# A margin for overtaking products in the order emitter, state-space tables stored in eight parts, attention loads held back: a hybrid S5 and forgetting-attention layer on one core

## The chip, the core and the metric

The kernel runs on one core of one Trainium2 chip. The metric is the device time of one execution in microseconds (us); several executions of each kernel are timed and the median is given. Beside them one execution was recorded by the hardware profiler, and every duration below comes from that record.

## What is computed

One decoder layer over 2048 tokens of 1024 channels, in float32. A projection of the normalized, modulated input gives the inputs of two branches and their gates; the branches are merged, projected, and normalized once more:

```python
u = _layer_norm(h) * (1.0 + scale[:, None, :]) + shift[:, None, :]
proj = u @ w_in[l]
(x_ssm, z_ssm, q, k, v, f_logit, z_attn, g_ssm, g_attn) = jnp.split(proj, split_idx, axis=-1)
y_ssm = _s5_mixer(x_ssm, ...)                  # 32 groups of 16 channels, 64 complex states each
y_ssm = (y_ssm * jax.nn.silu(z_ssm)) @ w_proj_ssm[l]
log_f = jax.nn.log_sigmoid(f_logit + b_f[l]).transpose(0, 2, 1)
o = _forgetting_attention(to_heads(q), to_heads(k), to_heads(v), log_f)   # 8 heads of 64, causal
y_attn = (o * jax.nn.silu(z_attn)) @ w_proj_attn[l]
merged = jax.nn.sigmoid(g_ssm) * y_ssm + jax.nn.sigmoid(g_attn) * y_attn
sub = (merged @ w_out[l]) * gate[:, None, :]
h = _layer_norm(DEEPNORM_ALPHA * h + sub, ln_g[l], ln_b[l])
```

## The kernel before

Every large product is made of three products of float32r parts (high by high, high by low, low by high), each of 128 x 128 weights by up to 512 columns. The stages follow one another on TensorE (PE): the layer norm, the modulation and the first projection columns (phase 1a); the other projection columns (`projections`), beside which the state-space branch runs on the other engines; attention in 64 rounds (8 heads by 8 pairs of query blocks, `scores`, `exponentials`, `weights_times_v`, `normalize`), beside which the GLU and the state-space output product run as filler (`background`); then the merge, the output projection and the last layer norm.

No engine reorders its instructions, so the order in which the program emits them decides. It is chosen by a rough clock, class `Model`: it keeps a modelled time of each engine (`M.t`), of the DMA queue (`M.t["dma"]`, filled at 360 bytes per ns, line 133) and of each tile's last write and reads. Each stage is a Python generator, a stream, that yields the modelled time at which its next step could start. `Model.merge` (line 168) goes through the streams in order of rank and takes the first whose time is not past PE's modelled clock; where there is none it takes the earliest and moves PE's clock there. State space ranks first, then the exponentials, `weights_times_v`, `normalize`, `scores`, then the end stages, `background` and `output`, and `projections` last. The lowest ranks are thus what fills PE while the higher ones wait. `scores` also waits until `background` has had a share of its 64 jobs (`share`, with `AHEAD = 62.5`), and runs at most three rounds ahead of `weights_times_v`.

Three ways of emitting matter here. `Engine.when` gives the modelled time of a step's operands. `Engine.soon` yields that time and then emits. `Engine.later` puts an instruction on a held list, from which it is emitted once PE's modelled clock has reached the time of its operands, or earlier where something needs it; `sp.dma_start` without `later` is emitted at once, and the SyncE queue (SP) then stands until the transfer's semaphores are there, with all later transfers behind it.

The state-space tables of all 32 groups are built in one tile `pk` by `ssm_params`, stored to `pk_sc` by a single transfer (line 963) and read back a group at a time into `pkg` tiles by `stage_l` (line 988). `stage_a` makes from them `CA` (VectorE, DVE), `G` and the phase tables (GpSimd, POOL); the first product that needs these is in `stage_b`, into a `bg` bank. `projections` empties its four `pp` banks through two `st` tiles that ScalarE (ACT) writes, for the z columns VectorE too, and SP stores (`zs_sc<-st`).

Attention's operands come from `load_keys` (line 1202: `ks`, `fb` and `vs` of 512 keys, a ring of six) and `load_q` (line 1215: the queries of two rounds, a ring of two). `pools` (line 1236) loads two chunks of keys and the queries of rounds 0 and 1 early; the rest is asked for by `scores`.

Of the kernel before, what the change touches and what calls it, by code (L numbers as in the profile page):

```python
# [8 lines left out]
F32 = mybir.dt.float32  # L9
# [9 lines left out]
NW = 4          # token windows of 512  # L19
WT = 512  # L20
KD = D // 128
NG = 32         # state-space groups
GH = 16         # channels of a group
CL = 8          # tokens of a chunk
NCH = S // CL   # chunks
CW = WT // CL   # chunks of a window
# [10 lines left out]
PKN = 163       # of a group: Bbar 16 | swapped 16 | C 16 | swapped 16 | tables 64 | powers 19 | A^7..A^0 16  # L37
# [4 lines left out]
class Model:  # L42
    """A rough clock of the engines, by which the order of emission is chosen (it computes no data)."""

    # from the end of an instruction to the start, on another engine (or the same), of one that needs it
    LAT = dict(pe=dict(dve=230, act=270, pool=260, pe=0), dve=dict(pe=190, act=150, pool=130, dve=125),
               act=dict(pe=190, dve=198, pool=110, act=0), pool=dict(pe=190, dve=155, act=175, pool=100))

# [31 lines left out]
    def deps(self, e, kw):  # L80
        """When the operands are there for engine e (whose own accesses are in order)."""
        rd, wt = self.aps(kw)
        r = 0.0
        for n in rd:
            if n in self.wr:
                end, by = self.wr[n]
                r = max(r, end + self.lat(e, by))
            for h in self.held:
                if n in h[2]:           # (a transfer that is still to come)
                    r = max(r, max(h[0] + 1100, self.t["sp"] + 1100, self.t["dma"]) + 1700)  # L90
        for n in wt:
            for by, end in self.ac.get(n, {}).items():
                if by not in (e, "in") or (by == "in" and e != "sp"):
                    r = max(r, end + self.lat(e, by))
            if e == "sp":
                r = max(r, self.ac.get(n, {}).get("sp", 0.0) + self.lat(e, e))
        return r
# [36 lines left out]
    def run(self, e, op, kw):  # L134
# [11 lines left out]
        for n in wt:  # L146
            # parts of a tile that transfers fill do not wait for each other
# [3 lines left out]
    def settle(self, rd, wt, dma=False):  # L151
        """Emit what is held and has to come before a read of rd and a write of wt (transfers may fill parts of a
        tile in any order)."""
# [14 lines left out]
    def merge(self, streams):  # L168
        """Emit from the first stream whose next step would not wait; streams come in order of rank."""
# [8 lines left out]
        while live:  # L178
# [13 lines left out]
            self.t["pe"] = max(now, best[0])  # L192
# [4 lines left out]
class Engine:  # L197
    """An engine whose instructions the model sees."""
# [14 lines left out]
    def when(self, **kw):  # L213
        """When an instruction with these operands could start."""
        d = self.m.deps(self.name, kw)
        return d if self.name in ("pe", "sp") else max(d, self.m.t[self.name])

    def soon(self, op, /, **kw):
        """A stream's step: the instruction, emitted once it would not wait."""
# [3 lines left out]
    def later(self, op, /, **kw):  # L223
        """The instruction, emitted once its operands are there (the streams go on meanwhile)."""
# [6 lines left out]
def hybrid_layer(ctx: ExitStack, tc: tile.TileContext, x, c, w_ada, b_ada, w_in, b_f, lam_re, lam_im,  # L231
# [32 lines left out]
    def pround(o, i):  # L264
        """Pool's copy into float32r (its rounding)."""
# [19 lines left out]
    # maskb[q, k] = 0 where k <= q, NEG elsewhere  # L285
# [4 lines left out]
    # ------------------------------------------------------------------ phase 1: input projection  # L290
    esl = ExitStack()               # left: until the projection is done
# [11 lines left out]
    def ps_tile(n=[0]):  # L303
        """One of four banks, which attention later has for scores (three) and outputs."""
# [7 lines left out]
    def bg_tile(n=None):  # L312
        if n is not None and n % 4 > 1:         # (the banks of the transposes, once attention is done)
# [6 lines left out]
    def bank():  # L320
        """Whichever of the two banks of bg_tile is free."""
# [12 lines left out]
    def split_wide(raw, n):  # L334
        """A stream that splits a chunk of weights; the tiles are there at once."""
# [8 lines left out]
    def rstd_of(p, mv, n):  # L344
        """1 / sqrt(var + eps) of the variances mv[:, :, 1]."""
# [21 lines left out]
    def until(f):  # L367
        """A condition to wait on, whatever the time."""
        return lambda: 0.0 if f() else None

    def modulation():
        """shift | 1 + scale of silu(c) @ w_ada + b_ada, as columns, 128 channels at a time."""
# [3 lines left out]
        act.activation(out=one, in_=ident[:, 0:1], func=AF.Sqrt)    # (its table is there when the layer norm needs it)  # L376
# [43 lines left out]
    def early_keys():  # L420
        """Two column tiles of the keys' weights, with which the first window goes on while the next one comes."""
# [7 lines left out]
    def modulation_columns():  # L429
        """Sums over the partitions, as columns."""  # L430
# [17 lines left out]
    def column_sums(acc, n, c0):  # L448
        """mods[:, c0:] = sums of acc over its partitions, as columns, + b_ada."""
# [34 lines left out]
    def normalized():  # L484
        """Windows of tokens, less their mean and over their spread."""
# [21 lines left out]
    def modulated():  # L507
        """u = normalized * (1 + scale) + shift, channels on partitions."""
# [28 lines left out]
    def low_parts():  # L537
        """The two parts of u."""
# [23 lines left out]
    def products_of(ps, w, hi, lo, c0):  # L562
        """A tile of columns of the projection of a window."""
# [7 lines left out]
    def store_parts(kind, m, w, ps):  # L571
        """Queries (scaled) or keys, in two parts."""
# [92 lines left out]
    # the other columns, with the state-space branch alongside  # L665
# [55 lines left out]
    def forget_bias():  # L721
        """f_sc[h, t] = cumulative log_sigmoid(f + b_f)."""
        with ExitStack() as es:
# [10 lines left out]
            # log1p(e) = 2 artanh(s), s = e / (2 + e) <= 1/3  # L734
# [25 lines left out]
    def gate():  # L760
        """The gate part of the modulation, as a row (scaled by 1/16, which the merge leaves)."""
# [17 lines left out]
    def ssm_params():  # L779
        """Per group: input and output matrices, powers and phases, written to pk_sc."""  # L780
        with ExitStack() as es:
            p0 = pl(es, "spp", side="right")
            pk = p0.tile([128, NG, PKN], F32, name="pk")
            uv = p0.tile([128, 4, NG], F32, name="uv")    # phase of A^8 (cos, sin), zoh (re, im)
# [22 lines left out]
            # cosine and sine of arg = n pi/2 + r  # L807
# [21 lines left out]
            od, ev = t32(), t32()       # quadrant: odd * sign, even * sign  # L829
# [7 lines left out]
            def lin(o, p0_, q0, p1, q1, sub):  # L837
                """o = p0 q0 +- p1 q1"""
# [10 lines left out]
            # 0..8: real A^k, both halves; 9..17: imaginary A^k, [-; +]; 18: |A|^8; 19, 20: phase of A^8  # L849
# [4 lines left out]
            den, am, cr, ci = t32(), t32(), t32(), t32()      # zero-order hold  # L854
# [51 lines left out]
            # input matrix: Bbar = zoh * B, and with its halves swapped  # L906
            with ExitStack() as es2:
# [15 lines left out]
                # output matrix as [state, group, channel], and with its halves swapped  # L923
# [12 lines left out]
            # phase tables: cos, sin of phase * b and of phase * 16 a for a, b in 0..15  # L936
            ta_ = [p0.tile([128, NG, 8], F32, name=f"ta{i}") for i in range(2)]
            u_ = [p0.tile([128, NG], F32, name=f"u{i}") for i in range(2)]
            for cc, ss in ((64, 80), (96, 112)):
# [4 lines left out]
                while n < 16:  # L944
# [10 lines left out]
                    # double the phase  # L955
# [7 lines left out]
            sp.dma_start(out=pk_sc.rearrange("g p n -> p g n"), in_=pk)  # L963

    sq = dict(a=0, b=0, c=0, d=0, e=0, r=0, x=0, t=0, ready=False, st={})
    esss = ExitStack()

    def side():
        """What runs beside the projections, up to the state-space groups."""
# [18 lines left out]
    def stage_l():  # L988
        """Loads of each group."""
        yield until(lambda: sq["ready"])  # L990
        p = sq["p"]
        for g in range(NG):
# [3 lines left out]
            yield sp.when(out=pk, b=xr)  # L996
# [4 lines left out]
    def stage_a():  # L1001
        """Powered matrices and phase tables of each group."""
        yield until(lambda: sq["ready"])
        p, sign = sq["p"], sq["sign"]
        for g in range(NG):
# [21 lines left out]
            # C A^k: rows re = Cr Ar - Ci Ai, rows im = -(Ci Ar + Cr Ai)  # L1027
# [5 lines left out]
            # A^(7-j) Bbar  # L1033
# [19 lines left out]
    def stage_b():  # L1053
        """Stationary matrices and inputs of each group, split."""
# [44 lines left out]
    def stage_t():  # L1099
        """The matrix within a chunk, its columns put in the order of the output's rows."""  # L1100
# [20 lines left out]
    def stage_c():  # L1121
        """Chunk inputs, and the scan over chunks in a frame that turns with the phase."""
# [23 lines left out]
    def stage_r():  # L1146
        """The states before each chunk, turned back, split."""
# [20 lines left out]
    def stage_d():  # L1168
        """Outputs of each group: gelu, doubled."""
# [21 lines left out]
    # attention's inputs: chunks of 512 keys, loaded ahead  # L1191
# [4 lines left out]
    def ring(shape, dtype, tag, n, size, early, p0, p1):  # L1196
        """Tile n of a ring, whose first places are in a pool that is there earlier."""
# [4 lines left out]
    def load_keys():  # L1202
# [7 lines left out]
        sp.dma_start(out=f32(ks), in_=k_sc[h, :, :, tk].rearrange("a d t -> (a d) t"))  # L1210
        sp.dma_start(out=fb, in_=f_sc[h:h + 1, tk].to_broadcast([128, 512]))
        sp.dma_start(out=f32(vs), in_=v_sc[h, tk, :].rearrange("(n p) e -> p n e", p=128))
        at["k"][h, j], at["v"][h, j], at["f"][h, j] = ks, vs, fb

    def load_q():
        """The queries of two rounds, on both halves of the partitions."""
# [4 lines left out]
        for hf in range(2):  # L1221
            sp.dma_start(out=f32(qd[hf * 64:(hf + 1) * 64]),
# [3 lines left out]
    # ------------------------------------------------------------------ phase 2: attention beside the GLU and the  # L1226
    # projections; phase 3: merge, output projection, layer norm
    esat, esb = ExitStack(), ExitStack()

    def pools():  # L1230
        """The room of the input projection goes to attention, that of the state space to what runs beside it."""
# [16 lines left out]
        atp = pl(esat, "atp", side="right")  # L1248
        done["at"] = done["bg"] = True
# [3 lines left out]
    WR = 10         # places of the ring of weight chunks  # L1253
    WE = 2          # of these, in the earlier pool
    ZT = 3          # places of the ring of what products are combined with
    ck = dict(tiles={}, jobs=0)

    def weight_chunks():
        """The chunks of w_glu (gate and value in turn), w_proj_ssm and w_proj_attn, split."""
# [27 lines left out]
    def free_place(raws):  # L1287
        """Whether a load takes the place of the earlier pool."""
# [502 lines left out]
```

## Time and profile before

| | us |
|---|---|
| median of 3 runs | 1916.91 (1913.0 to 1919.92) |
| profiled execution, first to last instruction | 1913.3 |
| PE busy in it | 1833.8 |
| DVE, POOL, ACT busy | 1082.5, 923.6, 775.1 |

Matmuls are pipelined, so PE's busy time counts them at the rate at which they could follow each other. The difference between span and busy time is time in which PE stood. Beside it the record has the granted TensorE clock, which is 1.0 at 2.4 GHz and 0.5 at 1.2 GHz; a busy stretch at 0.5 does half the work.

### The profile page before, as it was taken

How to read it: one execution, taken by the hardware profiler on the slowest of the kernel's cores; microseconds unless marked ns; L12 is line 12 of the kernel's file. 1: busy time of each engine (PE TensorE's matmuls, PEld its weight loads, DVE VectorE, ACT ScalarE, POOL GpSimd, SP SyncE). 2: the span in 40 equal slices, each digit the busy share in tenths (PEclk: the TensorE clock that was granted, in tenths of full speed). 3: DMA queues.
4: the chain of work that ended last, by engine and by line, in shares of the span. 5: the costliest groups of instructions: out<-in, count | busy, mean ns of one | idle time of the engine just before them, and what ended most of it. 6: DMA issues, size and time to landing. Idle time of an engine off the chain costs nothing. (4 is left out here: it accounts for less than half of the span.)

```text
span 1913.3 us, 30538 instructions
## 1 busy us (share of the span) xinstructions
PE 1833.8 (96%) x10104; PEld 1565.5 (82%) x10104; DVE 1082.5 (57%) x2886; ACT 775.1 (41%) x1849; POOL 923.6 (48%) x1343
## 2 busy tenths in 40 slices
PE   4999999998999999999998999999999999899997
PEld 3789988886787888888887888988889888788886
DVE  8651114734555555552004777876777866567666
ACT  5441111121433444443114767876767866311110
POOL 5222111113889999995306566376543436533110
PEclk9899999998999999999998999999999999999999
DMA  9434346654333333335217365265364543744432
GB/s 302 138 86 119 94 110 183 149 133 121 101 94 105 100 105 97 105 101 138 91 50 189 98 169 140 77 183 152 113 201 131 151 137 127 260 146 136 131 123 89
DMA packets 276915, 252.37 MB, mean 132 GB/s; under 512 B 66396, under 2 KB 211828, under 8 KB 276756
## 3 DMA queue, kind: packets, MB, share of 16 engines
q1 hardware_dynamic: 276756, 250.41, 45.7%
q8 instruction: 80, 1.31, 0.3%
q14 instruction: 79, 0.65, 0.1%
HBM read 159.50 MB, written 86.63 MB: 129 GB/s over the span
## 5 line engine op out<-in xcount | busy, mean ns | idle before, releaser
L209 PE MATMUL pp<-uh,hi 128*128 128x512 f32 x1136 | 451.0, 397 | 0.0
L209 PE MATMUL pp<-uh,lo 128*128 128x512 f32 x1136 | 446.0, 393 | 0.0
L209 PE MATMUL pp<-ul,hi 128*128 128x512 f32 x1136 | 445.1, 392 | 0.0
L209 ACT ACTIVATE st<-pp 128x512 f32<-128x512 f32 (+2 forms) x168 | 93.9, 559 | 439.1 <-PE pp L209 383.4
L209 DVE TENSOR_TENSOR pl<-pt,ph 128x512 fp32r<-128x512 f32 (+1 forms) x288 | 183.3, 657 | 122.3 <-ACT ph L209 121.7
L209 PEld LDWEIGHTS pp<-uh,lo 128*128 128x128 f32 x1136 | 214.2, 189 | 46.3
L209 PEld LDWEIGHTS pp<-uh,hi 128*128 128x128 f32 x1136 | 216.4, 190 | 41.5
L209 PEld LDWEIGHTS pp<-ul,hi 128*128 128x128 f32 x1136 | 214.7, 189 | 41.9
L209 ACT ACTIVATE srow<-srow,nm 128x512 f32<-128x512 f32 (+2 forms) x320 | 207.6, 653 | 0.4 <-DVE nm L209 0.3
L209 ACT ACTIVATE ph<-pt 128x512 fp32r<-128x512 f32 (+1 forms) x288 | 159.8, 572 | 64.4 <-PE pt L209 51.6
L209 DVE CUSTOM_DVE_ANT_0 srow<-sc,fb 128x512 f32<-128x512 f32 (+3 forms) x288 | 163.0, 594 | 21.9 <-PE sc L209 21.9
L209 PE MATMUL sc<-ks,qd 128*128 128x512 f32 (+2 forms) x640 | 163.7, 381 | 7.1 <-DMA qd<-q_sc 7.1
L209 PE MATMUL pt<-ident,srow 128*128 128x128 f32 x1088 | 159.3, 275 | 8.7 <-DVE pl L209 4.7
L209 PE MATMUL acc<-ph,vs 128*128 128x256 f32 x576 | 163.0, 308 | 2.5 <-POOL ph L209 2.5
L209 POOL TENSOR_TENSOR oo<-oo 64x256 f32<-64x256 f32 x128 | 93.7, 732 | 143.0 <-ACT oo L209 140.0
L209 POOL TENSOR_SCALAR hi<-raw 128x512 fp32r<-128x512 f32 x60 | 39.9, 665 | 237.8 <-PE pp L209 191.7
L209 PEld LDWEIGHTS pt<-ident,srow 128*128 128x128 f32 x1088 | 128.4, 141 | 27.2 <-DVE pl L209 9.5
L209 PE MATMUL acc<-pl,vs 128*128 128x256 f32 x576 | 147.4, 282 | 0.5 <-DVE pl L209 0.5
L209 PE MATMUL bg<-bh,wh 128*128 128x512 f32 (+1 forms) x384 | 140.2, 365 | 5.1 <-DVE zt L209 5.1
L209 PE MATMUL bg<-bh,wl 128*128 128x512 f32 (+1 forms) x384 | 138.1, 360 | 0.0
L209 PE MATMUL bg<-bl,wh 128*128 128x512 f32 (+1 forms) x384 | 137.8, 359 | 0.0
L209 PEld LDWEIGHTS sc<-ks,qd 128*128 128x128 f32 x640 | 107.9, 193 | 24.4 <-issue 8.4
(240 smaller groups left out, 3811.3 us busy)
## 6 DMA issues: line engine op xcount, KB each, us to landing
xt<-in_x_dram SPq DMA_DIRECT2D x32, 512.0 KB, 3.7
qd<-q_sc SPq DMA_DIRECT2D x64, 256.0 KB, 5.4
raw<-in_w_in_dram SPq DMA_DIRECT2D x30, 512.0 KB, 4.5
wada<-in_w_ada_dram SPq DMA_DIRECT2D x16, 512.0 KB, 7.0
k_sc<-st SPq DMA_DIRECT2D x32, 256.0 KB, 3.3
v_sc<-st SPq DMA_DIRECT2D x32, 256.0 KB, 2.3
q_sc<-st SPq DMA_DIRECT2D x16, 512.0 KB, 3.3
gs_sc<-st SPq DMA_DIRECT2D x32, 256.0 KB, 2.3
```

The source lines that it names most:

```text
L209: return fn(kw["out"], 0.0) if op == "memset" else fn(**kw)
```

## The change

The diff also deletes comments and docstrings, which emits nothing. What is left has three parts.

```diff
+    MARGIN = 300.0
...
-            self.t["pe"] = max(now, best[0])
+            self.t["pe"] = max(now, best[0] - self.MARGIN)
...
     def when(self, **kw):
         d = self.m.deps(self.name, kw)
-        return d if self.name in ("pe", "sp") else max(d, self.m.t[self.name])
+        if self.name == "pe":
+            return d + self.m.MARGIN
+        return d if self.name == "sp" else max(d, self.m.t[self.name])
...
             yield sp.when(in_=pk)
-            sp.dma_start(out=pk_sc.rearrange("g p n -> p g n"), in_=pk)
+            for i in range(0, NG, PKG):
+                sp.dma_start(out=pk_sc[i:i + PKG].rearrange("g p n -> p g n"), in_=pk[:, i:i + PKG])
+                sq["stored"].append(M.t["dma"] + 2500)
...
+    PKG = 4
...
     def stage_l():
-            yield sp.when(out=pk, b=xr)
+            yield max(sp.when(out=pk, b=xr), sq["stored"][g // PKG])
+            M.t["sp"] = max(M.t["sp"], sq["stored"][g // PKG])
             sp.dma_start(out=pk, in_=pk_sc[g])
...
     def load_keys():
-        sp.dma_start(out=f32(ks), ...)
-        sp.dma_start(out=fb, ...)
-        sp.dma_start(out=f32(vs), ...)
+        sp.later("dma_start", out=f32(ks), ...)
+        sp.later("dma_start", out=fb, ...)
+        sp.later("dma_start", out=f32(vs), ...)
...
     def load_q():
-            sp.dma_start(out=f32(qd[hf * 64:(hf + 1) * 64]),
+            sp.later("dma_start", out=f32(qd[hf * 64:(hf + 1) * 64]),
...
     def pools():
         bgp = pl(esb, "bgp")
         atp = pl(esat, "atp", side="right")
+        load_q()
+        load_keys()
+        load_keys()
         done["at"] = done["bg"] = True
```

A step on PE is counted as ready 300 ns after its modelled operands; if no step of any stream is ready, the earliest is taken and PE's modelled clock moves to 300 ns before its yielded time, for a PE step to the operands' own time. The tables are stored by eight transfers of four groups, and a group's load is emitted only when the modelled clock says that its part has been stored for 2.5 us. The transfers of attention go on the held list, and `pools` asks for the queries of rounds 2 and 3 and for two more chunks of keys when the room for them opens.

## Rows read from the trace of the kernel before

**Rows 1.** Page, first part: busy time, share of the span, instructions.

```profile
PE 1833.8 (96%) x10104; PEld 1565.5 (82%) x10104; DVE 1082.5 (57%) x2886; ACT 775.1 (41%) x1849; POOL 923.6 (48%) x1343
```

**Rows 2.** Busy time by stretch; columns as its head says.

```profile
core 0: us, PE busy (x) PEld busy (x) DVE busy (x) ACT busy (x) POOL busy (x), PEclk, DMA share, GB/s
0.00:57.00 57.00, 29.00 (x127) 23.19 (x128) 49.10 (x88) 27.76 (x55) 29.82 (x39) 0.90 0.97 277
...
459.00:467.40 8.40, 0.91 (x5) 0.41 (x3) 2.63 (x4) 0.90 (x2) 5.74 (x10) 0.69 0.49 150
467.40:472.40 5.00, 4.92 (x13) 3.64 (x14) 1.51 (x5) 1.19 (x3) 2.88 (x6) 0.50 0.11 33
...
1033.60:1039.00 5.40, 5.33 (x16) 4.38 (x17) 2.92 (x12) 0.00 (x0) 3.51 (x5) 0.50 1.14 235
1039.00:1619.50 580.50, 563.04 (x3608) 496.55 (x3607) 432.69 (x1403) 414.12 (x1038) 315.07 (x483) 0.99 0.50 142
1619.50:1656.00 36.50, 27.55 (x182) 26.00 (x181) 19.61 (x31) 13.43 (x27) 27.22 (x27) 0.91 0.80 261
```

**Rows 3.** Timelines, 459 to 468 us: start, duration, instruction, idle time and releaser.

```profile
467.48 0.40 PE L209 MATMUL bg<-CA,pkg 128*16 128x128 f32 x1 [7.58 <-DVE CA L209]
...
464.73 0.69 DVE L209 SCALAR_TENSOR_TENSOR st<-st,pp 128x512 f32<-128x512 f32 x1 [12.99 <-ACT st L209]
...
461.29 0.41 POOL L209 TENSOR_TENSOR G<-pkg 128x128 f32<-128x128 f32 x1 [12.48 <-DMA pkg<-pk_sc]
```

**Rows 4.** Timeline of SP's queue, 444 to 466 us.

```profile
444.78 0.37 SPq L209 DMA_DIRECT2D pk_sc<-pk  x1
445.21 7.70 SPq L209 DMA_DIRECT2D dsk<-in_ssm_d_dram  x1
459.33 0.33 SPq L209 DMA_DIRECT2D pkg<-pk_sc  x1
...
461.19 4.58 SPq L209 DMA_DIRECT2D zs_sc<-st  x3
```

**Rows 5.** DMA issues, 440 to 470 us: count, size each, us to landing.

```profile
pk_sc<-pk SPq DMA_DIRECT2D x1, 2608.0 KB, 14.5
...
dsk<-in_ssm_d_dram SPq DMA_DIRECT2D x1, 2.0 KB, 14.3
```

**Rows 6.** From 1013 us: PE's waits to 1039, SP's timeline, DMA to 1035.

```profile
PE sc L209 <- DMA qd<-q_sc: 7.1, 2, 6.9
...
1026.69 1.26 SPq L209 DMA_DIRECT2D qd<-q_sc  x2
...
DMA packets 6289, 4.90 MB, mean 223 GB/s; under 512 B 2635, under 2 KB 4751, under 8 KB 6287
```

**Rows 7.** PE's waits, 1039 to 1619 us: total us, times, longest.

```profile
PE pt L209 <- DVE pl L209: 4.7, 6, 1.2
PE pt L209 <- ACT srow L209: 3.8, 2, 3.4
PE acc L209 <- DVE lb L209: 3.1, 4, 1.4
PE acc L209 <- POOL ph L209: 2.5, 1, 2.5
PE acc L209 <- ACT srow L209: 1.4, 1, 1.4
PE acc L209 <- DVE mx L209: 1.3, 1, 1.3
PE acc L209 <- DVE pl L209: 0.5, 1, 0.5
```

**Rows 8.** One of three stretches of attention at half clock; columns as in Rows 2.

```profile
1114.10:1117.50 3.40, 3.40 (x10) 2.74 (x9) 3.33 (x7) 2.05 (x5) 3.40 (x4) 0.50 0.73 163
```

**Rows 9.** SP's waits, 1039 to 1619 us: total us, times, longest.

```profile
SPq L209 <- PE sc L209: 10.8, 14, 4.8
```

**Rows 10.** Filler alone (tile bg), last eight rounds: PE, PEld, DVE, ACT busy, PEclk, DMA.

```profile
1546.40:1619.50 73.10, 25.15 (x91) 16.06 (x91) 5.42 (x8) 0.00 (x0) 0.98 0.48 145
```

## What the change will do to the time

> **What bounds the kernel now.** I read the page's first part first: PE is busy in 1833.8 of 1913.3 us [rows 1]. No other engine comes near, and the change takes no product away, so all it can win is the 79.5 us in which PE stands and the time it runs at half clock. The table by stretch then says where these are [rows 2]: 28.0 us before 57 us, 7.5 at 459 to 467, 6.9 at the start of attention [rows 6], 17.5 inside attention (580.50 less 563.04), 9.0 where the merge begins (36.50 less 27.55), and most of the rest behind the last product. From 57 to 459 us PE never stands, because a projection product with old operands is always at hand.
>
> Each long stand also has a stretch at half clock behind it. After the one at 459 us the clock is 0.50 until 472.4, so 5 us of busy PE do 2.5 us of work; after the one at the start of attention, 5.4 us do 2.7 [rows 2]. Inside attention there are three windows of 3.4 us at 0.50 [rows 8], up to 1.7 us lost in each, 5.1 together. The whole sum in reach of the three edits is then 7.6 + 2.5, 6.9 + 2.7, and 17.5 + 5.1, some 42 us or 2.2%. The waits of PE, in a third view, say who ends each, and that decides how much an edit reaches.
>
> **Part 1, the tables in parts.** PE stands 7.58 us for `CA` of the first group [rows 3]. SP tells why: the store is issued at 444.78 and lands 14.5 us later [rows 4, 5]; the first `pkg` load waits in SP until 459.33, and the stores of z columns stand behind it until 461.19 [rows 4]. So the `st` tiles are full, ACT and then DVE get to their `st` step late (464.73), and `CA` comes behind that on DVE although POOL has had `pkg` since 461.29 [rows 3]. The emitter charged the store 2608 KB at 360 bytes per ns, 7.4 us, half of what it took; that is how PE came to `CA` too early.
>
> The change adds seven DMA issues at 0.37 us each on SP [rows 4], 2.6 us, in front of the `dsk` load and the z stores; two `st` tiles and four banks cover that, and without the cover it would cost its 2.6 us. It does not bring the first tables by much. The 2 KB `dsk` load, issued behind the store and waiting for nothing of it, took 14.3 us [rows 5], so what is issued behind the parts arrives behind all eight, at about 459.5. What it does bring is that SP no longer stands: z stores issued before the load pass at once. Then `st` is free near 461 and `CA` need not wait for 464.73. Bounds of the gain in idle time: nearly nothing below (the load lands with two z stores of 256 KB ahead of it, about 1.4 us each at the store's 184 bytes per ns, so PE stops waiting at about 466: 1.5 us gained), and all 7.6 above. Between them, `pkg` near 461.5 to 462 and POOL's three and DVE's three steps of about 2 us put `CA` at 464. PE comes to it a little later than now, since the emitter adds 0.3 us and sees its load behind the z stores (0.7 us each by its own rate), at about 461. That leaves 3 us of standing: 4.6 gained. A stand of that size is followed by one window of 3.4 us at 0.50 in attention [rows 8], not by 5 us of it behind a longer idle stretch, so 0.8 more. Part 1: -5.4 us.
>
> The Trainium skill, page "DMA: Bandwidth & Descriptors", section "Queues, rings and completion order", says that each engine consumes the descriptors of a ring in order. By that the first part is stored early and its load is still served last, which speaks against most of what storing in parts could give. The `dsk` row is this trace's sign of it, 14.3 us for 2 KB. If instead the load could pass the other seven parts, the whole stand and its slow stretch would go, -10.1 in place of -5.4.
>
> **Part 2, attention loads.** Holding them back would help if SP stood for their room. In attention SP's waits that PE's score products end come to 10.8 us in all, 14 times [rows 9], and none of PE's waits there is ended by a DMA [rows 7]. So `later` itself is costed at nothing, bounds -1 and +1; its cover is the lead of the loads, three rounds, and without it a load costs the 6 to 7 us of the start. The new loads in `pools` are another thing. PE stands 6.9 us there for the queries of rounds 4 and 5, issued at 1026.69, and the DMA moved 4.90 MB in the 22 us around it at 223 GB/s [rows 6]: the queue is full. The queries of rounds 2 and 3 and the first of the two chunks come where they came before. The second chunk, 0.79 MB, moves ahead of the y loads, the weight chunks, the zs loads and those queries, on SP (some 1.4 us of issues) and in the DMA queue: 0.79 MB at 223 GB/s is 3.5 us later for all of them. The emitter knows it as 2.2 us and adds 0.3, so PE comes to round 4 about 2.5 us later: +1.0 us. Bounds: -7 if what fills those 2.5 us lets the rest arrive, +4.5 with no filler (the weights it needs are late as well) and a longer slow stretch.
>
> **Part 3, the margin.** Inside attention PE waits 16 times, 17.4 us in all, mostly for DVE or ACT steps that come 0.3 to 3.4 us after the emitter expects them [rows 7]. A step now goes ahead of lower ranks only 0.3 us later, and in between stand scores or filler. Taken at its own size the margin takes 0.3 us off each wait, nothing off those already shorter: about 5.1 us over the 16 (the small ones count 0.1 to 0.3). Of the three slow windows half should go with the shorter waits, 2.5. Part 3 in attention: -7.6 us. Bounds: all 22.6 above; below zero, +5, since a new order puts other steps together and its waits are drawn anew; nothing in the trace excludes that. I take the value near the margin's own size because a DVE wait of 0.78 us in the mean (4.7 over 6) is longer than what is added.
>
> Elsewhere the margin is costed at nothing. In the first 57 us nothing else is at hand, as DVE is busy 49 of 57 us there [rows 2]. Beside the projections `projections` still fills. Where the merge begins, the 9.0 us hang on the end of the last round. Bounds for these together: -3 to +3. The state-space branch runs up to 1 us later, which only the last projections would see, and they hide it.
>
> **Sum.** -5.4 + 1.0 - 7.6 = -12.0 us. Against the profiled execution that is 1913.3 - 12.0 = 1901.3; the median of the runs shown is 3.6 us above it, and what makes that up is not touched, so 1916.9 - 12.0 = 1904.9.
>
> **The rivals.**
> *The waits of attention are only dealt anew.* Part 3 gives 0: -4.4, 1912.5. For it speaks that the waits have six kinds of releaser, and the longest (3.4, 2.5) are ten times the margin [rows 7].
> *The margin does more than its size.* A late DVE step delays the next, so slack at each hop ends whole trains of waits. Three quarters of 22.6 us go, and the start of attention stays as it is: -5.4 - 17 = -22.4, 1894.5. Against it speak the same long waits.
> *The parts do nothing*: the dependence is on the whole table, or the load is placed early anyway, and only 1.5 us are gained in part 1: -8.1, 1908.8.
> *Slower: the filler is spent too early.* In attention's last eight rounds filler is 91 products, 25.15 us of 73.1 [rows 10]. The margin takes filler where PE would not have stood; if half of that is gone by 1546 us, the rounds that end the stage lack 12.6 us of cover. With the late queries (+4.5) and nothing from attention's waits: -5.4 + 4.5 + 12.6 = +11.7, 1928.6. It decides from about four of the 64 jobs of lead lost to earlier rounds (91 products are 7.6 jobs of 12). Against it: `share` holds the scores back for the filler, so some is in excess now.
>
> **How the numbers follow.** Forecast 0.42, 1904.9, by itself 1899 to 1911; margin does more 0.16; parts do nothing 0.08; dealt anew 0.21; slower 0.13. A measurement of this kernel can tell about 0.3%, 5.75 us, from no change: 1911.2 to 1922.7. Faster: nine tenths of the forecast, the second and the third, 0.61. Same: the rest of the forecast and nearly all of the fourth, with a little of the slower case, 0.26. Slower 0.13. The range goes from 1892 (within the case of 1894.5) to 1921 (the dealt-anew case with +5 and a late start), leaving out the slower case and the far end of the better one.
>
> **What the profile after would show.** Part 1: eight stores, SP not standing behind them, `pkg` still not before 459.5 or so, and a stand of PE of about 3 us in place of 7.6; a stand of none would show that loads pass stores. Part 2: the stand for queries at the start of attention as long as now or a little longer. Part 3: waits inside attention near 12 us with fewer slow windows; 17 or more would prove the margin too small for its cause. Wrong most easily is part 3, whose size rests on an order of emission that no row shows.

## The result: slower by half a percent

The changed kernel takes 1928.46 us, median of 5 runs (1925.65 to 1930.07), against 1916.91 us: 1.0052 of the time before, 95% interval 1.0037 to 1.0067. The profiled execution spans 1927.6 us where it spanned 1913.3. I had forecast 1904.9.

The page of the kernel after, first part (busy us, share of the span, instructions), answers to [rows 1]:

```profile
PE 1839.0 (95%) x10104; PEld 1566.2 (81%) x10104; DVE 1085.3 (56%) x2886; ACT 773.1 (40%) x1849; POOL 928.6 (48%) x1343
```

The products are the same 10104. The stand at the first `CA`, which answers to [rows 3 to 5], in PE's and SP's timelines and the DMA issues:

```profile
468.11 0.61 PE L211 MATMUL bg<-CA,pkg 128*16 128x128 f32 x2 [8.41 <-DVE CA L211]
...
447.75 7.01 SPq L211 DMA_DIRECT2D pk_sc<-pk  x8
454.80 1.22 SPq L211 DMA_DIRECT2D dsk<-in_ssm_d_dram  x1
456.12 1.78 SPq L211 DMA_DIRECT2D zs_sc<-st  x1
457.94 0.48 SPq L211 DMA_DIRECT2D pkg<-pk_sc  x1
...
466.50 0.42 POOL L211 TENSOR_TENSOR G<-pkg 128x128 f32<-128x128 f32 x1 [19.07 <-DMA pkg<-pk_sc]
...
pk_sc<-pk SPq DMA_DIRECT2D x8, 326.0 KB, 10.6
```

SP no longer stands behind the store, and a z store passes at 456.12; but the first `pkg` load, issued at 457.94, is there for POOL only at 466.50, and PE stands 8.4 us where it stood 7.6. (Three traces below, `loads_only`, `oz_free` and `early_filler`, have PE's order of before up to here and stand 8.6, 9.2 and 9.4 us, so the 7.6 lies on the short side, and the stand did not grow beyond that spread.)

PE's waits at the start of attention (1013 to 1039 us, [rows 6]) and inside it (1039 to 1639 us, [rows 7]); total us, times, longest:

```profile
PE sc L211 <- DMA qd<-q_sc: 7.1, 2, 6.6
PE pt L211 <- ACT srow L211: 1.0, 1, 1.0
...
PE pt L211 <- DVE pl L211: 12.6, 10, 3.3
PE pt L211 <- ACT srow L211: 3.7, 2, 3.2
PE acc L211 <- DVE pl L211: 3.6, 8, 0.9
PE pt L211 <- DVE li L211: 1.9, 2, 1.6
PE sc L211 <- DVE mx L211: 1.2, 1, 1.2
PE sc L211 <- DMA ks<-k_sc: 0.4, 1, 0.4
PE acc L211 <- DVE lb L211: 0.3, 1, 0.3
```

The waits inside did not shrink from 17.4 us, they grew to some 24, 25 times in place of 16. Where they lie shows in the last eight rounds, up to the last attention product. The table by stretch with all instructions, before (from 1546.4 us) and after (from 1575.1 us), and under it the filler alone after, which answers to [rows 10]:

```profile
1546.40:1619.70 73.30, 69.43 (x443) 61.47 (x442) 52.01 (x163) 48.84 (x121) 39.47 (x60) 0.98 0.48 144
...
1575.10:1639.70 64.60, 54.06 (x354) 45.31 (x353) 48.08 (x156) 48.12 (x122) 36.77 (x58) 0.97 0.37 103
...
1575.10:1639.70 64.60, 0.17 (x2) 0.28 (x3) 0.00 (x0) 0.00 (x0) 0.97 0.37 103
```

Two filler products where there were 91, and these two stand behind the last attention product in PE's order: all 64 jobs are done before this stretch begins. PE is busy 54.06 of 64.60 us where it was busy 69.43 of 73.30. Its waits in these two stretches, before and then after:

```profile
PE pt L209 <- ACT srow L209: 3.4, 1, 3.4
PE acc L209 <- DVE lb L209: 0.4, 1, 0.4
...
PE pt L211 <- DVE pl L211: 5.1, 5, 1.8
PE pt L211 <- ACT srow L211: 3.2, 1, 3.2
PE acc L211 <- DVE pl L211: 1.7, 5, 0.6
PE sc L211 <- DMA ks<-k_sc: 0.4, 1, 0.4
```

They come to 10.4 us in place of 3.8, so all that the waits inside attention grew by lies here.

To compare kernels whose filler lies in other places I take attention apart by head. A head runs from the first `lb` transpose of its first round to that of the next head (the first from the first score product, the last to the end of the last `acc` product), and from its length I take 0.227 us for each filler product that starts in it, their spacing at full clock. In us net of filler:

```
head               1     2     3     4     5     6     7     8    sum
before          65.7  55.9  51.6  51.8  55.2  53.3  50.1  52.6  436.2
after           67.3  58.6  53.9  56.0  51.1  49.9  50.8  64.2  451.7
```

Each row is one execution. Four traces with the same products in the same order in attention (before, and `parts_only`, `direct` and `charged` below) differ by up to 2.1 us in a head and 4.4 us in the sum, so smaller differences say nothing.

Attention got 15.5 us longer for the same work, 11.6 of them in the last head. Of these 11.6, 6.6 are the waits above; most of the rest is busy time of PE net of filler, 53.6 us in place of 48.8, which no run takes further apart. The rest of the 14.3 us between the two spans nearly cancels: what follows attention takes 1.3 us less beside the filler's 19 products.

### The profile page after: what moved, and what is told of

Read it like the earlier page. It is cut to its first block, busy times and chain, and to the rows that moved or that the text cites. A ratio compares the mean times of both kernels' runs of the same rounds, so it can differ in the third digit from the quotient of the medians.

```text
span 1927.6 us, 30508 instructions
## 1 busy us (share of the span) xinstructions
PE 1839.0 (95%) x10104; PEld 1566.2 (81%) x10104; DVE 1085.3 (56%) x2886; ACT 773.1 (40%) x1849; POOL 928.6 (48%) x1343
## 5 line engine op out<-in xcount | busy, mean ns | idle before, releaser
L211 PE MATMUL pt<-ident,srow 128*128 128x128 f32 x1088 | 160.1, 276 | 19.5 <-DVE pl L211 12.6
L211 DVE CUSTOM_DVE_ANT_0 srow<-sc,fb 128x512 f32<-128x512 f32 (+3 forms) x288 | 163.2, 595 | 11.7 <-PE sc L211 11.6
```

Source lines behind the costliest of these rows:

```text
L211: return fn(kw["out"], 0.0) if op == "memset" else fn(**kw)
```

## The experiments

Each time is compared with that of the kernel before on the same chip; a trace of the kernel before exists from the first chip alone. The parts first, each alone on the kernel before.

### The margin alone

```diff
+    MARGIN = 300.0
...
-            self.t["pe"] = max(now, best[0])
+            self.t["pe"] = max(now, best[0] - self.MARGIN)
...
-        return d if self.name in ("pe", "sp") else max(d, self.m.t[self.name])
+        if self.name == "pe":
+            return d + self.m.MARGIN
+        return d if self.name == "sp" else max(d, self.m.t[self.name])
```

> The kernel before with the margin of 300 ns alone; tables and attention loads as before. Theory F (the margin spends the filler early): in the emitted order the 64 filler jobs are used up by round 57 as in the changed kernel (64.0 there, 55.8 before), so the last eight rounds run without cover and the time is 1926 us, +9, with most of the added time after the start of round 56. Rival W (the waits of attention are only dealt anew and the loss comes from the table store and the new loads): 1917, within 4 us of before. My prediction's part 3 had 1909.

Measured 1.0075 (1.006 to 1.009), +14.4 us on 1920. The last head takes 64.5 us, with 8 filler products in it. That is more than theory F asked: head 4 also lost 10 us (62.1), to which the store experiment below comes back.

### The table store in parts alone

```diff
-            sp.dma_start(out=pk_sc.rearrange("g p n -> p g n"), in_=pk)
+            for i in range(0, NG, PKG):
+                sp.dma_start(out=pk_sc[i:i + PKG].rearrange("g p n -> p g n"), in_=pk[:, i:i + PKG])
+                sq["stored"].append(M.t["dma"] + 2500)
...
-            yield sp.when(out=pk, b=xr)
+            yield max(sp.when(out=pk, b=xr), sq["stored"][g // PKG])
+            M.t["sp"] = max(M.t["sp"], sq["stored"][g // PKG])
```

> The kernel before with the tables stored in eight parts alone. Theory Q (a load issued behind the parts is served behind all of them): TensorE stands 7 to 8.5 us for the first group's CA as before, the first pkg load lands some 8 us after its issue, time 1917 us, within 2 of before. My prediction's part 1 had 1911.5, a stand of 3 us.

Measured 0.9979 (0.9967 to 0.9991), -4 us; the stand is 8.22 us. The expected stand came, the time is better than expected: in the trace the clock is at 0.50 from 462.7 to 469.5 us, where it was so from 462.1 to 472.4 before, and attention begins 2.0 us earlier. The interval of the time, -1.7 to -6.3 us, holds these 2 us; more than that I can't place.

### The attention loads alone

```diff
-        sp.dma_start(out=f32(ks), ...)     # fb, vs and qd likewise
+        sp.later("dma_start", out=f32(ks), ...)
...
         atp = pl(esat, "atp", side="right")
+        load_q()
+        load_keys()
+        load_keys()
```

> The kernel before with the attention loads held back and the two extra chunks and queries asked for at the start alone. Theory: SP did not stand for their room, so the held list changes nothing, and the extra chunk of keys delays the queries of rounds 4 and 5 by up to 3.5 us: 1918 us, +1, with a wait for qd at the start of attention of 7 to 9 us. If the loads are what made the changed kernel slower: 1925 or more.

Measured 1.0026 (1.0008 to 1.0045), +5 us. PE's wait at the start of attention (1014 to 1041 us):

```profile
PE sc L209 <- DMA qd<-q_sc: 10.4, 2, 9.5
```

PE waits 3.3 us more for the queries than before; the 0.79 MB of extra keys take 3.5 at the prediction's rate, and no filler stands against it. Heads 3 and 4 took another 5.3 and 3.7 us more. So neither this nor the parts is the loss by itself. The three alone add up to some 15 us where all three together give 10; the four intervals, of 2 to 4 us to either side, leave open whether the parts of the change add.

### The filler: taken early without a margin, held back with it, spent sooner

The kernel before with more filler forced in front of the scores:

```diff
-            return AHEAD * (36 * h + p_ * (p_ + 1) / 2) / (36 * NH) - 3
+            return min(63.0, AHEAD * (36 * h + p_ * (p_ + 1) / 2) / (36 * NH) - 3)
...
-    AHEAD = 62.5
+    AHEAD = 74
```

> The kernel before, no margin, with one number changed: the share of filler that the scores wait for rises from 62.5 to 74 jobs, capped at 63, so that in the emitted order all 64 jobs are done by round 57, as in the changed kernel (55.8 before). Theory F (a missing filler is what costs): the last eight rounds take some 64 us in place of 53 net of filler, the rest stays, so +11: 1929 us. Rival W (the margin's order costs, not the filler): 1918, as before.

Measured 1.0163 (1.0144 to 1.0182), +31 us. The bare last head came, 67.4 us, 14.8 more than before (11 were expected). I missed that forcing scores to wait costs the other heads too, 19 us together.

The changed kernel with a ceiling beside the floor that `share` is:

```diff
+    def held_back():
+        r = done.get("qk", 0)
+        return r < len(rounds) and ck["jobs"] >= share(r) + 3 + LEASH
...
+    LEASH = 0
...
-                yield until(lambda: live["bg"] == 0 and (side_q or live["zt"] < ZT))
+                yield until(lambda: live["bg"] == 0 and (side_q or live["zt"] < ZT) and not held_back())
```

(and the same in front of the second product's jobs)

> The changed kernel, all three parts, with one addition: a filler job is not started while the jobs done are past their even share for the next round of scores, so that in the emitted order 56.0 jobs are done at round 57 in place of 64.0, and the filler lasts to the last round. Theory F: the last eight rounds get back some 12 us, 1916 us (1912 to 1919). If the loss lies in the margin's order as such (rival W): 1925 or more, as without the leash.

Measured 1.0021 (1.001 to 1.0033), some six tenths of the way back. The last head fell from 64.2 to 51.7, the 12.5 us of theory F, but head 7 rose by 8.3 and held a wait of 4.5 us. That filler is short at the end is shown; that it is the whole loss is not, for the time stayed outside the 1912 to 1919 us that were expected.

Other sizes of the margin, alone, by the one number `MARGIN`:

> The kernel before with a margin of 600 ns alone. In the emitted order the filler is used up at round 48, eight rounds sooner than with 300 ns. Theory F: two heads run bare at 11 us each, +22 on before: 1940 us, with 12 us or so more in each of heads 7 and 8 and not in the others. Rival W (a larger margin covers late operands better, the loss comes from elsewhere): less than the 1.0075 of the margin of 300.

Measured 1.0046 (1.003 to 1.0063), less than the margin of 300 and far from the 1940 us of theory F; in the time alone rival W has it. Filler alone by stretch, heads 7 and 8:

```profile
1509.50:1574.10 64.60, 0.00 (x0) 0.00 (x0) 0.00 (x0) 0.00 (x0) 0.97 0.44 118
1574.10:1636.60 62.50, 0.20 (x2) 0.31 (x3) 0.00 (x0) 0.00 (x0) 0.97 0.29 82
```

Both heads are bare and take 64.6 and 62.0 us net, 14.5 and 9.4 more than before, as theory F expected. But the heads that still had filler came down: 51.4, 50.0, 51.7, 56.4, 49.8 in heads 2 to 6, 259.3 together where before had 267.8. The margin does gain, where there is filler to pay for it.

> The kernel before with a margin of 100 ns alone. In the emitted order 57.0 filler jobs are done at round 57 (55.8 before), so the last head keeps its filler. Theory F: no cost of that kind, 1918 us, with the waits of attention dealt anew within 5 us either way. My prediction's reckoning (the margin's own size off each of 16 waits): 1916. If any margin costs by its order: 1924 or more.

Measured 1.004 (1.0022 to 1.0057), +7.7 us, with filler to the end and a last head of 52.2. Theory F said that no more than 5 us would be dealt, and the line on record for a cost by the order itself, 1924 us or more, was passed. Something else was dealt.

### The late output stores

In the margin of 100 I followed each long wait of PE back link by link. One of them, in SP's, ScalarE's, VectorE's and PE's timelines:

```profile
1116.02 1.34 SPq L211 DMA_DIRECT2D qd<-q_sc  x2
1117.42 0.59 SPq L211 DMA_DIRECT2D ks<-k_sc  x1
1118.10 0.38 SPq L211 DMA_DIRECT2D fb<-f_sc  x1
1118.52 0.54 SPq L211 DMA_DIRECT2D vs<-v_sc  x1
1119.17 1.10 SPq L211 DMA_DIRECT2D oz_sc<-oo  x1
...
1126.61 0.99 ACT L211 ACTIVATE oo<-acc 64x384 f32<-64x384 f32 x2 [4.68 <-DMA oz_sc<-oo]
1127.50 0.71 ACT L211 ACTIVATE srow<-srow,nm 128x512 f32<-128x512 f32 x1
...
1128.33 1.08 ACT L211 ACTIVATE ph<-pt 128x512 fp32r<-128x512 f32 x2
...
1128.96 1.29 DVE L211 TENSOR_TENSOR pl<-pt,ph 128x512 fp32r<-128x512 f32 x2 [5.94 <-ACT ph L211]
...
1129.71 0.55 PE L211 MATMUL pt<-ident,srow 128*128 128x128 f32 x3 [3.85 <-DVE pl L211]
```

PE waits for DVE's `pl`, which waits for ACT's `ph`, which stands in ACT's queue behind the copy of an earlier round's output into `oo`; and that copy waits 4.68 us for the store of the round two before it, because `oo` has two places. The store was issued behind two query and three key transfers and took some 7 us. ACT's waits of this kind are in every kernel that has the stores of before, 19.8 to 40.6 us in all; after (1039 to 1639 us), and the margin of 100 (1039 to 1643 us):

```profile
ACT oo L211 <- DMA oz_sc<-oo: 32.7, 8, 6.3
```

```profile
ACT oo L211 <- DMA oz_sc<-oo: 32.2, 7, 7.2
```

Before has them too, 26.0 us, 6 times. Only part of them reach PE: the expectations below count 4.6 us of PE's waits behind them before, 8.1 after and 13.5 with the margin of 100. The edit takes away what makes ACT wait:

```diff
-            za = T(atp, [64, 256], F32, tag="za", bufs=2, name="za")
+            za = T(atp, [64, 256], F32, tag="za", bufs=3, name="za")
...
-            fd = T(atp, [128, 2, 128], F32, tag="fd", bufs=3, name="fd")
+            fd = T(atp, [128, 2, 128], F32, tag="fd", bufs=2, name="fd")
...
-            yield from pool.soon("tensor_mul", out=v, in0=v, in1=za)
-            sp.later("dma_start", out=oz_sc[...], in_=v)
+            yield from pool.soon("tensor_mul", out=za, in0=v, in1=za)
+            sp.later("dma_start", out=oz_sc[...], in_=za)
```

> The kernel before with one thing changed in attention: the last product of a round's output is written to the gate tile za (three of them, fd two in place of three) and stored from there, so ScalarE's copy into oo no longer waits for the store of two rounds ago. Theory S (the long waits of attention are ScalarE standing for a late oz_sc store, its rounds-old transfer being queued behind keys and queries): two such waits, 1.2 and 3.4 us with a slow window, go: 1914 us, -5 on before. If such waits only move to another place: within 3 us of before.

> The kernel with the margin of 100 ns alone, with the same freeing of oo. In its trace six waits of 1.1 to 3.9 us, 13.5 in all, come behind a copy into oo that stood for a late store. Theory S: 12 us off the margin of 100, which was 1.0040 of before: 0.998 of before, 1916 us. Rival D (any new order deals the waits anew, whatever the stores): 1.002 to 1.006.

> The changed kernel with the same freeing of oo. Its trace has three such waits, 1.6, 3.3 and 3.2 us. Theory S with theory F: 7 us off 1.0052 of before, so 1.0015, 1921 us; the last eight rounds, without filler, stay at 60 us or more net. If F alone holds: 1.005 as before. If S explained all: below 0.997.

> The changed kernel with the filler held to its share (leash0) and the freeing of oo. In the trace of leash0 four waits of 1.5, 2.1, 4.5 and 1.9 us stood for a late store. Theories F and S together: 9 us off leash0's 1.0021, 0.9975 of before, 1913 us. Rival D: 1.002 or more.

Measured 0.9962 (0.9947 to 0.9977), 0.9934 (0.9914 to 0.9954), 0.9979 (0.9967 to 0.9992) and 0.996 (0.994 to 0.9979). All four are faster than before, the margin of 100 by 20 us against itself and the changed kernel by 14. The class of wait is gone from ACT's list in the margin of 100 (1039 to 1616 us), and its two largest are waits for PE itself:

```profile
ACT oo L211 <- PE acc L211: 97.1, 59, 5.0
ACT ph L211 <- PE pt L211: 51.1, 82, 3.8
```

So rival D, that any new order loses, falls, and the four gains (some 7, 20, 14 and 12 us) speak for theory S. They are larger than the waits counted, though, and the edit also changes PE's order in attention, which no run keeps apart. Then the margin of 300 alone with `oo` freed, which separates the margin from the other two parts:

> The kernel with the margin of 300 ns alone and oo freed from the late stores; tables and attention loads as before. Filler used up at round 56. Theories F and S: heads 2 to 7 net of filler come to some 309 us as in the changed kernel with oo freed (oz_free alone 320.9), the bare last head stays at 62 us (49.4 in oz_free): the margin's gain of 12 and its price of 13 cancel, 0.997 of before. If the margin costs by its order: the heads with filler are no better than oz_free's, 1.003.

Measured 0.9964 (0.995 to 0.9978). By heads, in us net of filler:

```
head               1     2     3     4     5     6     7     8    sum
oz_free         66.7  59.5  51.9  55.1  52.1  51.2  51.0  49.1  436.6
m100_oz_free    64.6  52.6  50.7  53.6  56.1  51.6  50.2  49.5  428.8
m300_oz_free    66.0  51.4  51.5  52.8  50.1  50.7  49.9  61.5  433.9
after_oz_free   67.9  52.9  51.0  53.2  50.0  50.6  50.6  62.6  438.7
```

This is the plainest answer of the study. The margin of 300 takes 14.5 us out of heads 2 to 7 (320.8 to 306.3) and gives 12.4 back in head 8. Head 4, which lost 10 us under the margin alone, takes 52.8. The freeing alone does not show in these sums (436.6, before 436.2): its 7 us are measured against executions of the kernel before on its own chip (1920.9 us), and the trace of before is from the first chip (1916.9 us).

### The first stand: what the emitter charges

Two edits on the kernel before. The first sends the tables and x of the first two groups straight to their places, ahead of the store:

```diff
+            for g in range(2):
+                sp.dma_start(out=sq["first"][g], in_=pk[:, g, :])
+                sp.dma_start(out=sq["xfirst"][g], in_=x_sc[g * GH:(g + 1) * GH].rearrange("h j c -> (h j) c"))
             sp.dma_start(out=pk_sc.rearrange("g p n -> p g n"), in_=pk)
...
```

(and `stage_l` takes these tiles for the first two groups)

> The kernel before, no part of the change, with the tables of the first two groups and their x copied straight to their places ahead of the one large store, so that no load of the first groups has to come behind it. Theory Q (the stand at the first CA is the queue behind the store): the stand of 7.6 us and the half clock behind it go, TensorE stands under 1.5 us there, 1909 us, -9. If the stand had another cause (the st tiles, the order on VectorE): it stays at 5 us or more, 1916.

Measured 0.9993 (0.9981 to 1.0006): nothing. PE's, ACT's, DVE's and POOL's timelines:

```profile
467.38 0.55 PE L209 MATMUL bg<-xh,ih 128*128 128x256 f32 x1 [6.77 <-DVE il L209]
473.02 0.58 PE L209 MATMUL bg<-xl,ih 128*128 128x256 f32 x1 [5.09 <-POOL xl L209]
...
465.72 0.60 ACT L209 ACTIVATE st<-pp 128x512 f32<-128x512 f32 x1 [13.96 <-DMA zs_sc<-st]
...
465.03 0.28 DVE L209 COPY kd<-bg 16x128 f32<-16x128 f32 x1 [12.56 <-DMA pk_sc<-pk]
...
465.17 0.62 POOL L209 TENSOR_TENSOR tta<-pkf 128x256 f32<-128x256 f32 x1 [16.15 <-DMA pk_sc<-pk]
```

The `CA` product, at 449.73, no longer waits, and the next products of the same group wait 11.9 us instead. By the profile DVE and POOL now stand 12.56 and 16.15 us for the table store itself, and ACT 13.96 us for a z store issued behind it, with the group's steps behind all three. Freeing one thing that waits for a store frees nothing while the next steps wait for the same store. The second edit moves no transfer:

```diff
             sp.dma_start(out=pk_sc.rearrange("g p n -> p g n"), in_=pk)
+            M.t["dma"] += 7100
```

> The kernel before, one line added to the emitter alone: after the store of the tables its clock of the DMA queue is moved on by 7.1 us, so the store is charged the 14.5 us it took and not 7.4. In the emitted order the first CA product moves from place 2173 on TensorE to 2209, 36 products of 0.227 us or 8.2 us of projection work later; nothing is stored or loaded otherwise. Theory C (the stand comes from the emitter's charge, not from the form of the store): the stand of 7.6 us falls under 1.5 us and its half clock goes, -9: 0.9955 of before. If SP standing behind the store is the cause: the stand stays at 4 us or more, -3 at most.

Measured 0.9929 (0.9909 to 0.9949), -13.6 us. In SP's timeline the load still stands until the store has landed; PE's timeline and the table by stretch:

```profile
458.55 0.33 SPq L209 DMA_DIRECT2D pkg<-pk_sc  x1
...
466.58 0.39 PE L209 MATMUL bg<-CA,pkg 128*16 128x128 f32 x2 [0.26 <-DVE CA L209]
...
457.00:477.00 20.00, 19.74 (x91) 15.92 (x90) 6.83 (x16) 3.96 (x9) 13.49 (x21) 1.00 0.47 132
```

PE comes to `CA` after 36 more projection products and waits 0.26 us, at full clock. The tables arrive no sooner behind their store (its load is issued 15.5 us after it, 14.6 before). That it was the emitter's charge is thereby shown, and that SP's stand cost anything by itself is not. The gain is some 3 us more than the stand and the slow clock of the trace before (7.6 and 2.5 us, 10.1 together); its interval, -9.8 to -17.4 us, holds these too.

### Together

`m100_oz_charged` is `m100_oz_free` with the `charged` line; the other two add to the freed `oo` a margin of 200 with parts, each part charged twice, and a margin of 300 with `LEASH = 2` and the `charged` line.

> Margin of 100 ns, oo freed, one store charged at 14.5 us. The order in attention is that of m100 with oo freed (0.9934); theory C takes the first stand away: -9 more, 0.9885 of before. If the stand stays: 0.993.

> Margin of 200 ns, oo freed, tables in parts, each part charged twice its bytes by the emitter; attention loads as before. Filler lasts to round 62 in the emitted order, the first CA product stands at place 2224. F, S and C together: -14 of m100 with oo freed (0.9934) with a last head of 51 to 54, and -9 for the first stand: 0.988 of before. If the margin has nothing left to take beyond 100 ns: 0.990. If F holds already at 63.5 jobs by round 62: 0.993.

> The kernel with the margin of 200 ns, oo freed, tables in parts and each part charged twice its bytes, once more, for its trace and a narrower interval: 0.986 of before. Theory F: with filler to round 62 the last head stays under 55 us net of filler; theory C: no stand over 1.5 us at the first CA.

> Margin of 300 ns, oo freed, one store charged at 14.5 us, and filler held to two jobs past its even share, so that in the emitted order 58 jobs are done at round 57 and 63.8 at round 62. F: the last head comes back from 61 to 50 us, and heads 2 to 7, which keep two jobs of lead, stay near 307 us: 0.985 of before. If the leash only moves the lack of filler into the other heads, as it did for leash0's head 7: 0.991.

Measured 0.9889 (0.9873 to 0.9906); 0.9858 (0.9834 to 0.9882) and again 0.9862 (0.9847 to 0.9876); 0.989 (0.9869 to 0.9912). The margin of 200 is the fastest kernel of the study, 1890.5 us against 1917.2 on its chip. Its last head holds filler (tile bg alone, 1536.2 us to the end of attention):

```profile
1536.20:1602.40 66.20, 17.38 (x66) 11.56 (x66) 4.79 (x7) 0.00 (x0) 1.00 0.53 158
```

and takes 51.4 us net; all heads come to 426.5, and PE waits 0.72 us at the first `CA`. With the leash the heads come to the same 426.9, heads 2 to 7 to 308.6 as expected and the last to 53.0 (50 were), though its time is no better than that of the margin of 100.

## Why the prediction was wrong

The step that failed most is in part 3: its sum takes 0.3 us off each wait and has no term for the filler that the margin spends on that. In place of -7.6 us attention took 15.5 more, 11.6 of them in a last head that has no filler. Part 1 was mis-sized as well: attention began no earlier.

- *What bounds the kernel, and what is in reach.* Right: the products stayed, and the differences that I could place are PE standing or its clock. With a smaller margin, parts charged at their time, and `oo` freed, 26.7 of the 42 us could be had.
- *Part 1, forecast -5.4.* The stand, put at 3 us, was 8.4 in the changed kernel and 8.2 with the parts alone. That loads are served behind all parts was right; the term that failed is when that is. The 2 KB load behind the parts was put at 459.5 and landed at 466.0 (454.80 and 11.2 us), so `pkg`, put at 461.5 to 462, was there at 466.5: 3.0 us of this are the later issue of the store (447.75 for 444.78), the rest its slower landing. PE was put at `CA` at 461 and came at 459.7, as before (459.9); in its order `CA` stands six products later than before, with the parts alone six earlier. That the emitter's half charge brings PE there too early stood in my own text, and I costed SP's stand instead; the `charged` run shows that the charge was the term. That the parts alone measure -4, near the forecast, is luck.
- *Part 2, forecast +1.0.* The delay was right (3.5 us said, 3.3 measured alone), the 2.5 us of filler against it were not there; alone the loads measure +5, partly in heads 3 and 4. In the changed kernel the wait for the queries is 7.1 us, as long as before, since there the margin (5.1 us by itself) pays for the delay. `later` itself has no run of its own.
- *Part 3, forecast -7.6.* The step "the margin's own size off each wait" failed. (It was summed wrongly too: sixteen times 0.3 us is 4.8 at most and not 5.1, and rows 7 name five kinds of releaser, not six.) I took PE's waits at their first link, a DVE step some tenths late. Behind the long ones that I followed stood ACT's wait for the `oz_sc` stores, 26.0 us before, a view that I did not open; a margin of 0.3 us does not cover 3 to 7 us. With the stores out of the way, the margin's gain in heads 2 to 7 is 14.5 us, above my 7.6, and the bare last head takes 12.4 of it back.
- *The slower rival.* It named the mechanism that ended the race: filler spent by round 56, at a price of 12.6 us; 11.6 were measured in head 8. Its time, 1928.6, is that of the result, partly by luck: its -5.4 for part 1 came out at nothing and its +4.5 for the start at +1.5 (head 1), errors that in part cancel. I gave it 0.13 because `share` holds the scores back for the filler. That is a floor under the filler and no ceiling, and the margin is a standing order to take filler: its lead over `share` grew from some 4 jobs to 12.
- *Dealt anew.* Also true, as the margin of 100 (+7.7) and the loads alone show, and in these orders worse than zero. As I read it, what is dealt is which products meet the late stores; no run shows this product by product.

## What to carry to other kernels

Work that fills waits is a budget: count it to the end of the stage before asking a scheduler to be more careful, since what it takes early is missing where nothing else is left. Follow each long wait back until the link that is late by its own size, usually a transfer; a margin covers tenths of a microsecond, not a store behind a queue of loads. And where a planner's charge for one step is off by half, correct the charge before changing the step.

## What was not expected of the hardware

A store of 64 KB takes 1.9 to 7.1 us to land in attention, in the kernel before as after (median 3.3 and 3.2); the one followed above, issued behind two query and three key transfers, took some 7.

Eight stores of 326 KB, back to back, held SP for 7.0 us, 0.9 us each, where the single one of 2608 KB took 0.37 us of SP. But the 2 KB load issued right behind the single store held SP for 7.70 us [rows 4], and 1.22 us behind the eight, so with store and load together SP was held for 8.1 and 8.2 us, and not 2.6 us longer as I had added up. What holds it, no run separates.
